# Holding back the first output stores until the input loads are through, in a 3x3 convolution

## Chip, cores, metric

The kernel runs on one core of one Trainium2 chip; the other cores are idle. The metric is the device time of one execution in microseconds (us). The "span" of a profile runs from the first to the last instruction and is about 1.8 us shorter than the device time of the same run. The "granted clock" is the share of its full speed at which TensorE was allowed to run. HBM is the chip's large memory, SBUF the memory beside the engines, and PSUM the one that TensorE writes its products to. For a program on one core, a run is called slow when it is over 1.5% above the fastest run of the same kernel; ratios use the other runs, called fast.

## The reference

A convolution of 16 images, 64 input channels, 64x64 pixels, with 128 output channels and a 3x3 kernel, in fp32, zero padding. The weights are 90% zeros, but neither kernel uses that.

```python
batch, c_in, h, w, c_out, k = 16, 64, 64, 64, 128, 3
for b in range(batch):
    for co in range(c_out):
        for ci in range(c_in):
            for kh in range(k):
                for kw in range(k):
                    output[b, co] += weight[co, ci, kh, kw] * x_pad[b, ci, kh:kh+h, kw:kw+w]
```

Input 16.8 MB, output 33.6 MB: every byte has to cross between HBM and SBUF once.

## The kernel before

Images go in pairs (64 channels each fill 128 partitions). All eight pairs are loaded up front by GpSimd, cast to bf16 on the way; the first half of pair 0 (the "head") comes as fp32 by the sync queue and is cast on chip, so that TensorE can start early. Before it, 27 matmuls of zeros keep TensorE busy.

```python
xs = [x_pool.tile([128, H, W], BF16, name=f"x{p}") for p in range(NP)]
w_sb = const_pool.tile([C_OUT, C_IN * KH * KW], FP32, name="w_sb")
nc.sync.dma_start(out=w_sb, in_=weight.rearrange("o i kh kw -> o (i kh kw)"))
x_head = o_pool.tile([128, H, W], FP32, name="o")            # o_pool: 7 buffers of 16 KiB per partition
nc.sync.dma_start(out=x_head[:, 0:HEAD, :], in_=pair(0)[:, 0:HEAD, :])
nc.gpsimd.dma_start(out=xs[0][:, HEAD:H, :], in_=pair(0)[:, HEAD:H, :])
...
for p in range(1, NP):
    nc.gpsimd.dma_start(out=xs[p], in_=pair(p))
...
for _ in range(27):
    nc.tensor.matmul(idle_ps, idle_rhs, idle_rhs, start=True, stop=True)
```

A block is 16 rows of a pair. GpSimd adds neighbouring rows ("row sums", s), TensorE makes 6 + 24 products, ScalarE copies the shared ones out of PSUM, and VectorE (DVE) adds them to the rest into the output buffer. After a pair's four blocks two stores of 2 MiB are issued.

```python
def twos(p, o, r0):
    s = s_pool.tile([128, 8, W], BF16, name="s")              # s_pool: 3 buffers
    nc.gpsimd.tensor_tensor(out=s, in0=..., in1=..., op=ADD)
    shared = product([(s, G1, 0, 1)], 8)
    ...
    for first, terms in ((r0, even), (r0 + 1, odd)):
        ps = product(terms, 8)
        for n in range(2):
            nc.vector.tensor_tensor(out=o[n][:, first : r0 + 16 : 2, :], in0=ps[n], in1=pc[n], op=ADD)

for p in range(NP):
    o = [o_pool.tile([C_OUT, H, W], FP32, name="o") for _ in range(2)]
    ...                                                       # four blocks; the last pair stores in halves
    if not last:
        for n in range(2):
            nc.sync.dma_start(out=out[2 * p + n], in_=o[n])
```

## Time and profile before

| | before |
|---|---|
| device time | 127.76 us, median of 3 (127.69 to 127.97) |
| span of the profile | 125.4 us (this run took 127.12 us) |
| TensorE busy | 107.5 us (86%), matmuls to 110.4 us |
| VectorE, GpSimd, ScalarE busy | 66%, 32%, 31% |
| DMA engines | 8 or 9 tenths busy in all slices but the first and the last |
| stores issued | 18, the first at 21.6 us, the last at 111.8 us |

### The profile page before, as it was taken

Reading aid. Unit: us, or ns where it says so; the run is one execution under the profiler, and the core shown is the slowest. Engines: PE = TensorE matmul, PEld = TensorE weight load, DVE = VectorE, ACT = ScalarE, POOL = GpSimd, SP = SyncE. Lnnn points to the kernel's source line nnn. Section 1 sums busy time; section 2 is a strip of 40 time slices with the busy share of each in tenths; the row PEclk is TensorE's granted clock in tenths of the full one; section 3 lists DMA queues with packets and bytes.
Section 4 is the critical chain, followed back from the end, with each engine's and each line's share of the span. In section 5 each row is a group of like instructions: output and inputs, shape, how many; then the busy total and the mean of one; then the engine's idle time right before and its main releaser. Section 6 shows DMA issues by size and latency. Waiting matters only on the chain.

```text
span 125.4 us, 2486 instructions
## 1 busy us (share of the span) xinstructions
PE 107.5 (86%) x1002; PEld 58.8 (47%) x1002; DVE 82.4 (66%) x135; ACT 39.0 (31%) x71; POOL 40.7 (32%) x45
## 2 busy tenths in 40 slices
PE   6679999999999999999999999999999999920000
PEld 6435555555555555555555555555555555500000
DVE  0463877877787778777877787778777877760000
ACT  4555323333333333333333333333333333300000
POOL 6936533333333333333333333333333300000000
PEclk9999999999999999999999999999999999997555
DMA  5999999989999999999999999999999999999980
GB/s 146 338 222 220 212 214 220 191 259 350 324 311 337 308 293 319 342 316 308 426 429 423 408 429 434 450 416 434 418 418 429 429 444 423 434 397 423 423 369 10
DMA packets 4044, 42.93 MB, mean 342 GB/s; under 512 B 448, under 2 KB 448, under 8 KB 704
## 3 DMA queue, kind: packets, MB, share of 16 engines
q1 hardware_dynamic: 2880, 34.90, 66.2%
q0 software_dynamic: 1152, 7.86, 30.7%
q8 instruction: 8, 0.13, 0.4%
q14 instruction: 4, 0.03, 0.1%
HBM read 17.07 MB, written 33.55 MB: 404 GB/s over the span
## 4 chain that ended last, share of the span: by engine, by line
PE 81%; DMA 4%; DVE 1%; issue 1%; DVEq 0%; SPq 0%
PE ps L135 81%; DMA o<-in_x_dram 4%; DVE o L168 1%; DVEq L214 0%; DVE x L87 0%; SPq L60 0%; DVEq L168 0%
## 5 line engine op out<-in xcount | busy, mean ns | idle before, releaser
L168 DVE TENSOR_TENSOR o<-ps,pc 128x512 f32<-128x512 f32 x124 | 77.8, 686 | 22.1 <-PE ps L135 19.8
L135 PE MATMUL ps<-x,wT 64*128 64x504 bf16 (+3 forms) x780 | 88.8, 373 | 1.5 <-DVE x L87 1.5
L135 PEld LDWEIGHTS <-wT 64*128 64x128 bf16 x966 | 55.2, 94 | 49.4 <-issue 1.5
L154 POOL TENSOR_TENSOR s<-x 128x512 bf16<-128x512 bf16 x31 | 35.6, 1152 | 57.7 <-PE ps L135 41.5
L161 ACT COPY pc<-ps 128x512 f32<-128x512 f32 x62 | 33.3, 589 | 64.0 <-issue 61.8
L135 PE MATMUL ps<-s,wT 64*128 64x512 bf16 (+1 forms) x186 | 25.7, 377 | 0.0
L74 PE MATMUL ps<-idle_rhs 128*128 128x128 bf16 x27 | 3.1, 310 | 1.0 <-DVE idle_rhs L71 1.0
L67 POOL DMA_DIRECT2D x<-in_x_dram x7 | 3.7, 561 | 0.0
L74 PEld LDWEIGHTS <-idle_rhs 128*128 128x128 bf16 x27 | 2.8, 144 | 1.0 <-DVE idle_rhs L71 1.0
L91 DVE CAST w_bf<-w_sb 128x192 bf16<-128x192 f32 (+1 forms) x4 | 1.3, 382 | 3.0 <-DMA w_sb<-in_weight_dram 3.0
L149 DVE COPY o<-ps 128x512 f32<-128x512 f32 x2 | 1.4, 692 | 2.0 <-PE ps L135 2.0
L148 ACT COPY o<-ps 128x512 f32<-128x512 f32 x2 | 1.2, 586 | 2.4 <-PE ps L135 2.4
L87 ACT CAST x<-o 128x576 bf16<-128x576 f32 (+1 forms) x2 | 1.5, 802 | 0.5 <-DMA o<-in_x_dram 0.5
L91 ACT ACT_TABLE_LOAD x1 | 1.3, 1283 | 0.7 <-PEq L203 0.7
L97 PE MATMUL ps<-ident,w_bf 128*128 128x128 bf16 x9 | 1.1, 292 | 0.4 <-DVE w_bf L91 0.4
L87 DVE CAST x<-o 128x576 bf16<-128x576 f32 x1 | 0.5, 460 | 1.4 <-DMA o<-in_x_dram 1.4
L91 ACT CAST w_bf<-w_sb 128x64 bf16<-128x64 f32 (+1 forms) x2 | 0.7, 418 | 1.9 <-DMA w_sb<-in_weight_dram 1.9
L97 PEld LDWEIGHTS <-w_bf 128*128 128x128 bf16 x9 | 0.8, 128 | 0.8 <-DVE w_bf L91 0.8
L101 DVE TENSOR_TENSOR wT<-ps,wT 128x384 bf16<-128x384 f32 x2 | 1.0, 550 | 0.0
L63 POOL DMA_DIRECT2D x<-in_x_dram x1 | 0.7, 696 | 0.8 <-POOLq L203 0.8
L71 DVE MEMSET idle_rhs<- 128x64 uint32 x1 | 0.1, 112 | 0.8 <-PEq L203 0.8
L110 ACT CAST wT<-ps 128x384 bf16<-128x384 f32 x1 | 0.5, 481 | 0.4 <-PE ps L97 0.4
(8 smaller groups left out, 1.9 us busy)
## 6 DMA issues: line engine op xcount, KB each, us to landing
out_dram<-o SPq DMA_DIRECT2D x14, 2048.0 KB, 19.8
x<-in_x_dram POOLq DMA_DIRECT2D x7, 1024.0 KB, 29.3
out_dram<-o SPq DMA_DIRECT2D x4, 1024.0 KB, 12.3
o<-in_x_dram SPq DMA_DIRECT2D x1, 1024.0 KB, 5.4
x<-in_x_dram POOLq DMA_DIRECT2D x1, 512.0 KB, 7.5
w_sb<-in_weight_dram SPq DMA_DIRECT2D x1, 288.0 KB, 3.1
```

Source lines behind the costliest of these rows:

```text
L67: nc.gpsimd.dma_start(out=xs[p], in_=pair(p))
L74: nc.tensor.matmul(idle_ps, idle_rhs, idle_rhs, start=True, stop=True)
L87: copy(out=xs[0][:, a:b, :], in_=x_head[:, a:b, :])
L91: copy(out=w_bf4[:, g, a:b, :], in_=w_v[:, k : k + b - a, :])
L97: nc.tensor.matmul(wps[:, j, :], src, ident, start=True, stop=True)
L101: nc.vector.tensor_tensor(out=wT[:, g], in0=wps, in1=wT[:, G1], op=SUB)
L135: nc.tensor.matmul(ps[n][:, lo:hi, c_lo:c_hi], tap(g, kw, n), src[q, a:b:step, c_lo + kw - 1 : c_hi + kw - 1], start=(i == 0), stop=(i == ...
L148: nc.scalar.copy(out=o[0][:, r0 : r0 + rows, :], in_=ps[0])
L149: nc.vector.tensor_copy(out=o[1][:, r0 : r0 + rows, :], in_=ps[1])
L154: nc.gpsimd.tensor_tensor(out=s, in0=xs[p][:, r0 : r0 + 16 : 2, :], in1=xs[p][:, r0 + 1 : r0 + 16 : 2, :], op=ADD)
L161: nc.scalar.copy(out=c, in_=shared[n])
L168: nc.vector.tensor_tensor(out=o[n][:, first : r0 + 16 : 2, :], in0=ps[n], in1=pc[n], op=ADD)
```

## The change

The intent: let the loads have the DMA engines to themselves first, and only then the stores. The stores of pairs 0 and 1 are held; the first of them gets an artificial dependency on the last addition of the second block of pair 2 (pairs are counted from 0), and the others stand behind it on the sync queue. As three pairs must now fit on chip before the first store, there are eight output buffers instead of seven. The room comes from putting the fp32 weights into the unused half of the head's buffer and from having two row-sum buffers instead of three.

```diff
--- before.py
+++ after.py
@@ -42,9 +42,9 @@
 
     const_pool = ctx.enter_context(tc.tile_pool(name="const", bufs=1))
     x_pool = ctx.enter_context(tc.tile_pool(name="x", bufs=1))
-    s_pool = ctx.enter_context(tc.tile_pool(name="s", bufs=3))
+    s_pool = ctx.enter_context(tc.tile_pool(name="s", bufs=2))
     p_pool = ctx.enter_context(tc.tile_pool(name="pc", bufs=4))
-    o_pool = ctx.enter_context(tc.tile_pool(name="o", bufs=7))
+    o_pool = ctx.enter_context(tc.tile_pool(name="o", bufs=8))
     psum_pool = ctx.enter_context(
         tc.tile_pool(name="psum", bufs=8, space=bass.MemoryType.PSUM)
     )
@@ -56,10 +56,12 @@
         return x[2 * p : 2 * p + 2].rearrange("n i h w -> (n i) h w")
 
     xs = [x_pool.tile([128, H, W], BF16, name=f"x{p}") for p in range(NP)]
-    w_sb = const_pool.tile([C_OUT, C_IN * KH * KW], FP32, name="w_sb")
+
+    first_buf = o_pool.tile([128, H, W], FP32, name="o")
+    x_head = first_buf[:, 0:HEAD, :]
+    w_sb = first_buf.rearrange("p h w -> p (h w)")[:, HEAD * W : HEAD * W + C_IN * KH * KW]
     nc.sync.dma_start(out=w_sb, in_=weight.rearrange("o i kh kw -> o (i kh kw)"))
-    x_head = o_pool.tile([128, H, W], FP32, name="o")
-    nc.sync.dma_start(out=x_head[:, 0:HEAD, :], in_=pair(0)[:, 0:HEAD, :])
+    nc.sync.dma_start(out=x_head, in_=pair(0)[:, 0:HEAD, :])
     nc.gpsimd.dma_start(out=xs[0][:, HEAD:H, :], in_=pair(0)[:, HEAD:H, :])
     ident = const_pool.tile([128, 128], BF16, name="ident")
     make_identity(nc, ident)
@@ -165,9 +167,18 @@
         for first, terms in ((r0, even), (r0 + 1, odd)):
             ps = product(terms, 8)
             for n in range(2):
-                nc.vector.tensor_tensor(
+                done = nc.vector.tensor_tensor(
                     out=o[n][:, first : r0 + 16 : 2, :], in0=ps[n], in1=pc[n], op=ADD
                 )
+        return done
+
+
+
+    HELD = 2
+    held = []
+
+    def store(p, n, o, a, b):
+        return nc.sync.dma_start(out=out[2 * p + n][:, a:b, :], in_=o[n][:, a:b, :])
 
     for p in range(NP):
         o = [o_pool.tile([C_OUT, H, W], FP32, name="o") for _ in range(2)]
@@ -175,17 +186,30 @@
         for blk in range(4):
             r0 = 16 * blk
             if BLOCKS[p][blk] == "T":
-                twos(p, o, r0)
+                done = twos(p, o, r0)
             else:
                 for r, rows in ((r0, 8), (r0 + 8, 8)):
                     direct(p, o, r, rows)
             if last and blk % 2 == 1:
                 for n in range(2):
-                    rows = slice(r0 - 16, r0 + 16)
-                    nc.sync.dma_start(out=out[2 * p + n][:, rows, :], in_=o[n][:, rows, :])
-        if not last:
+                    store(p, n, o, r0 - 16, r0 + 16)
+            if p == HELD and blk == 1:
+                first = store(*held[0])
+                tc.add_manual_dep(
+                    first.ins,
+                    done.ins.name,
+                    mybir.DependencyInfo(
+                        mybir.DependencyClass.Sync, mybir.DependencyReason.DATA
+                    ),
+                    reason="loads first",
+                )
+                for args in held[1:]:
+                    store(*args)
+        if p < HELD:
+            held += [(p, n, o, 0, H) for n in range(2)]
+        elif not last:
             for n in range(2):
-                nc.sync.dma_start(out=out[2 * p + n], in_=o[n])
+                store(p, n, o, 0, H)
 
 
 # ---- launch: one core; inputs and outputs as the reference has them ----
```

## The prediction

> **What bounds the kernel now.** I read the chain of work that ended last first, because it names an engine, and then the slices, because they say whether that engine reaches the end of the span. The columns of the first two lines are shares of the span.
>
> ```profile
> PE 81%; DMA 4%; DVE 1%; issue 1%; DVEq 0%; SPq 0%
> PE   6679999999999999999999999999999999920000
> DVE  0463877877787778777877787778777877760000
> DMA  5999999989999999999999999999999999999980
> GB/s 146 338 222 220 212 214 220 191 259 350 324 311 337 308 293 319 342 316 308 426 429 423 408 429 434 450 416 434 418 418 429 429 444 423 434 397 423 423 369 10
> ```
>
> The chain puts 81% on the matmuls of line 135, but it stops at 111.8 us, with the last DVE addition and the last store's issue, while the span is 125.4 us. In the last four slices (each 3.13 us) PE and DVE are at 0 and the DMA row is still at 9. So the last 12 us are stores draining. The DMA row is at 8 or 9 from the second slice to the last but one: the 16 DMA engines never run dry after the first 3 us. I take the DMA queue as the bound and PE as second, some 12 us behind.
>
> The GB/s row seems to say otherwise: 215 at first, 320 in the middle, 427 late. The load queue writes bf16 and is counted by the bytes that it writes, while it reads fp32. The queues in four stretches show it (8 to 22, 22 to 26, 26 to 60 and 64 to 110 us; packets, MB, share of the 16 engines' time; q0 carries the loads that cast, q1 the stores):
>
> ```profile
> q0 software_dynamic: 411, 3.02, 103.4%
> ...
> q0 software_dynamic: 99, 0.68, 99.8%
> q1 hardware_dynamic: 3, 0.05, 2.9%
> ...
> q1 hardware_dynamic: 489, 7.23, 50.7%
> q0 software_dynamic: 483, 3.56, 50.1%
> ...
> q1 hardware_dynamic: 1339, 19.58, 100.0%
> ```
>
> Counting a load's bytes twice (fp32 read), loads alone move 2 x 3.02 MB / 14 us = 431 GB/s. Loads and stores mixed move (2 x 3.56 + 7.23) / 34 = 422. Stores alone move 19.58 / 46 = 426. The rate is thus the same whatever the mix, and only the total counts. The one worse stretch is 22 to 26 us, just after the first store is issued at 21.6 us: (2 x 0.68 + 0.05) / 4 = 353 GB/s. Against 431 that is 0.31 MB short, or 0.7 us. The trace's packet records show load packets of 0.62 us stretching to 0.8 to 1.3 us there, and the first store packet only at 25.8 us, 4.2 us after its issue.
>
> **What the Trainium skill says.** "DMA: Bandwidth & Descriptors", section "Where 436 GB/s comes from", gives the 16 SBUF ports a ceiling of 435.2 GB/s. The trace agrees: 422 to 431 in the three steady stretches, so there is almost nothing left to gain in rate. The same page, "Issuing engines are not separate DMA queues", says that DMAs from the sync and gpsimd engines run on the same 16 engines and interleave; the trace agrees with 50.7% and 50.1% for the two queues while both have work. Holding the stores back then frees the loads but does not shorten the sum. "SBUF — State Buffer", section "SBUF size: 192, 224, or 256?", gives about 208 KiB usable per partition. The eight inputs take 64 KiB, eight output buffers 128, the four fp32 copies 8, two row sums 2, and the constants some 5.5 (0.25 + 0.25 + 1.5 + 3.75, rounded): 208. That is why the weights move into the first output buffer and one row-sum buffer goes. No timing follows from it, and no run here shows the limit.
>
> **The change part by part.**
> 1. Row sums in two buffers. GpSimd's addition of 1152 ns (31 of them) can start once the shared product two blocks back has read its buffer. That product is the first 6 matmuls of a block, done about 0.83 us into it (the timeline shows 6 in 0.83 us). So the sum is ready about 0.83 + 1.15 + 0.1 = 2.1 us into block k for block k+2. A block lasts 12.8 us / 4 = 3.2 us (stores of successive pairs are issued at 34.35 and 47.15 us), so it is wanted at 6.4 us. 4.3 us of slack: cost 0.
> 2. Weights in the output buffer. The weight load and the head of x go to disjoint columns of one tile. That disjoint regions of a tile do not wait for one another shows today: the casts write rows 0 to 31 of the first input at 6.6 us, and its lower half, loaded by another DMA, lands only at 1.24 + 7.5 = 8.7 us. So the start should not move: PE at 7.1 us, and cost 0.
> 3. Eight buffers. Buffer reuse moves from three and a half pairs back to four. Pair 4 first writes at about 61.1 us. If the stores begin at 43 us, pair 0's 4.19 MB are out at 43 + 9.8 = 53, with a couple of us for the receipt 55. Pair 5 (73.9 us) needs pair 1, out at 63 to 65; pair 6 (86.7) pair 2, at 72 to 75; pair 7 (99.5) pair 3, at 82 to 84. No wait, slack 6 us or more; PE should still end at 110.4 us.
> 4. The held stores. Pair 0 has three blocks of sums and pair 1 four, so the addition that releases the first store is number 12 + 16 + 8 = 36 of line 168. In the DVE timeline:
>
> ```profile
> 38.76 2.52 DVE L168 TENSOR_TENSOR o<-ps,pc 128x512 f32<-128x512 f32 x4 [0.73 <-PE ps L135]
> 42.00 2.52 DVE L168 TENSOR_TENSOR o<-ps,pc 128x512 f32<-128x512 f32 x4 [0.73 <-PE ps L135]
> ```
>
> It ends at 38.76 + 2.52 = 41.3 us, so the first store is issued at 41.3 instead of 21.6. The loads meanwhile have the engines alone. By 22 us they have moved 3.59 of 7.86 MB. The other 4.27 MB at 3.02 / 14 = 0.216 MB per us take 19.8 us, so the loads end at about 41.8 us, and a little later with the stragglers (in the packet records some engines run 0.5 us behind), instead of 61.8. They were not late before: PE ran without a gap from 7.1 us on, and GpSimd waited for a load once, 2.2 us. Nothing is bought by having them earlier.
>
> Then only stores: 33.55 MB / 0.426 = 78.8 us. The end of the stream is the time of the first store byte plus 78.8 us. That first byte lies between 41.3 + 1.1 = 42.4 us (the first load is issued at 0.74 us and its first packet is at about 1.85, queue empty) and 41.3 + 4.2 = 45.5 us (the latency seen behind a full load queue). The loads run out just then, so I choose near the low end, 43.2 us: end of the stream at 122.0 us. Today's stream ends at 121.9 in the mean (120 us, then 2 us at 87%, then 3.4 us at 5%), with one straggling engine to 123.7. The sum: the 0.7 us handover slump goes away or shrinks, a gap of about 1 us between loads and stores comes in its place, and the mixing loss (422 against about 428 over 34 us, 0.5 us at most) goes as well. **Net about 0**, 127.8 us.
>
> **The rivals.**
> - A, an idle gap. If the first store needs its 4.2 us whatever the load queue does, the engines idle from 42 to 45.5 us, and the stream ends at 45.5 + 78.8 = 124.3, 2.4 us later: 130.1 us. For it: 4.2 us is the only store latency that can be read, as all later stores queue behind others. Against it: about six load packets of 0.62 us ahead in each engine would explain 3.7 us of it, and the first loads took 1.1 us.
> - B, separate streams are better. If mixing is what costs, the slump of 0.7 us and the mixed loss of 0.5 us are both saved, and the store stream starts at 42.4: 126.6 us. For it: the slump is real. Against it: more than that cannot come, since the total of 50.6 MB at 431 is 117.4 us and the engines are already busy nearly all the time.
> - C, PE becomes the end. It would if a buffer or the weights' shared tile stalled it: a false wait of the weight casts for the head of x (lands at 6.6 us, weights at 3.9) would push PE and thus the release back by up to 2.7 us, and the gap would grow by as much: 130 us. Against it: point 2.
>
> **Range and chances.** The middle is 127.8. Rival B gives the low side, so 126.9; the high side takes two thirds of rival A, so 129.3. Faster by over 2% (under 125.2 us) would take more than all idle and mixed loss that I can count: 0.03. Slower by over 2% (over 130.3 us) takes the full gap plus something: 0.06. Within 2%: 0.91.
>
> **What would show it.** Right: slices with 210 to 220 GB/s to about 42 us, then 427 to the end, without a 320 stage; first store issued at 41.3; PE without a gap and its end at 110.4; the DMA end within 1 us of 122. Rival A: one slice near 41 to 45 us with a DMA share well under 9. Rival C: DVE or PE waiting for the weights or for stores, and PE's start later than 7.1 us. The prediction is wrong if stores alone right after the loads run at a rate clearly off 426, or if the slowest engine's straggling (1.5 us today) changes much.

## The result and the profile after

| | before | changed |
|---|---|---|
| device time, same rounds | 127.77 us median of 6 (127.63 to 129.78) | 129.51 us median of 6 (128.87 to 133.74) |
| ratio of fast runs | 1 | 1.013, 95% interval 1.009 to 1.017 |
| span of the profile | 125.4 us | 128.0 us |
| first store issued | 21.6 us | 43.8 us |

A ratio is the mean time of one kernel's fast runs over the mean of the other's fast runs of the same rounds, so it is not quite the ratio of the medians in the table; the slowest run of each kernel here (129.78 and 133.74 us) is slow by the rule above and left out of it. The changed kernel is 1.3% slower. The forecast was 127.8 us with a range to 129.3: the time is outside of it, though only by 0.2 us, and "within 2%" came true.

These lines are of the page of the changed kernel: busy tenths of PE, granted TensorE clock and busy tenths of the DMA engines in 40 slices of 3.2 us, what the DMA engines moved (loads counted by the bf16 bytes that they write), and the chain of work that ended last (DVEq and SPq are the sequencers of VectorE and of the sync queue).

```profile
PE   6659999999999999999999999999999999920000
...
PEclk9985999999999999999999999999999999999555
DMA  4999999999999399999999999999999999999970
GB/s 119 356 227 210 210 225 215 212 207 230 212 210 215 123 415 410 410 410 456 428 410 410 425 456 415 404 415 430 448 410 425 410 456 415 425 392 417 425 315 15
...
PE 81%; DMA 5%; DVE 1%; issue 1%; DVEq 0%; SPq 0%
```

Three things differ from the lines of before. The DMA row has a 3 in the fourteenth slice (41.6 to 44.8 us), with 123 GB/s: a hole. The GB/s row has no 320 stage any more: about 215 to the hole, then about 425. And the clock row has an 8 and a 5 in the third and fourth slice. The chain is again PE with 81% and again says nothing on the end, which is 14 us of draining stores.

The queues of the changed kernel, from 8 to 42 us and from 46 to 110 us (packets, MB, share of the 16 engines' time):

```profile
q0 software_dynamic: 1002, 7.30, 102.8%
...
q1 hardware_dynamic: 1854, 27.05, 100.2%
```

The loads alone move 2 x 7.30 MB / 34 us = 429 GB/s, the stores alone 27.05 / 64 = 423, against 431 and 426 before. Then four stretches of 2 us around the hole in the changed kernel; the last three columns are the granted clock, the DMA share and GB/s:

```profile
core 0: us, PE busy (x) PEld busy (x) DVE busy (x) ACT busy (x) POOL busy (x), PEclk, DMA share, GB/s
40.00:42.00 2.00, 2.00 (x22) 0.99 (x18) 1.27 (x3) 0.97 (x2) 1.15 (x1) 1.00 0.96 201
42.00:44.00 2.00, 2.00 (x22) 1.01 (x20) 1.74 (x3) 0.86 (x2) 0.77 (x1) 1.00 0.15 33
44.00:46.00 2.00, 2.00 (x22) 1.05 (x20) 1.54 (x3) 0.21 (x1) 0.38 (x1) 1.00 0.82 344
46.00:48.00 2.00, 2.00 (x22) 1.03 (x20) 1.27 (x3) 1.07 (x2) 1.15 (x1) 1.00 1.06 442
```

From 42 to 44 us the engines are 15% busy, then 82%: about 2 x 0.85 + 2 x 0.18 = 2.1 us of all 16 engines are lost. The packet records say that the last load packet ends at 43.4 us (on the slowest engine; most are done by 42.3) and that the first store packet starts at 44.68 us. All compute engines work on in this time. And the release comes late. This is the DVE line of the additions, the fourth of which frees the first store, in the changed kernel:

```profile
41.22 2.52 DVE L170 TENSOR_TENSOR o<-ps,pc 128x512 f32<-128x512 f32 x4 [0.72 <-PE ps L137]
```

It ends at 41.22 + 2.52 = 43.7 us, where the same addition of the profile before ended at 41.3. The 2.5 us are there from the start of the kernel on. The first real matmuls, before:

```profile
7.12 3.99 PE L135 MATMUL ps<-x,wT 64*128 64x512 bf16 x36 [1.54 <-DVE x L87]
10.93 0.83 PE L135 MATMUL ps<-s,wT 64*128 64x512 bf16 x6
```

and changed:

```profile
7.90 5.67 PE L137 MATMUL ps<-x,wT 64*128 64x512 bf16 x36 [2.39 <-DVE x L89]
13.39 0.83 PE L137 MATMUL ps<-s,wT 64*128 64x512 bf16 x6
```

The second line of each is the first matmul of the next block, and it starts 2.46 us later in the changed kernel (13.39 against 10.93). Of this, 0.78 us is the later start, as the matmuls wait for the cast of the head (7.90 against 7.12). The other 1.68 us is in the 36 matmuls themselves, which spread over 5.5 instead of 3.8 us: the clock record has half clock from 8.78 to 12.19 us, 3.41 us in which half the speed costs 1.7 us.

### The profile page after: what moved, and what is told of

Its sections match the earlier page's. It is cut to its first block, busy times and chain, and to the rows that moved or that the text cites. A ratio compares the mean times of both kernels' runs of the same rounds, so it can differ in the third digit from the quotient of the medians.

```text
span 128.0 us, 2487 instructions
## 1 busy us (share of the span) xinstructions
PE 109.2 (85%) x1002; PEld 57.3 (45%) x1002; DVE 82.3 (64%) x135; ACT 38.9 (30%) x71; POOL 40.8 (32%) x45
## 3 DMA queue, kind: packets, MB, share of 16 engines
HBM read 17.07 MB, written 33.55 MB: 396 GB/s over the span
## 4 chain that ended last, share of the span: by engine, by line
PE 81%; DMA 5%; DVE 1%; issue 1%; DVEq 0%; SPq 0%
PE ps L137 81%; DMA o<-in_x_dram 5%; DVE o L170 1%; DVEq L238 0%; DVE x L89 0%; SPq L63 0%; DVEq L170 0%
## 5 line engine op out<-in xcount | busy, mean ns | idle before, releaser
L137 PE MATMUL ps<-x,wT 64*128 64x504 bf16 (+3 forms) x780 | 90.3, 379 | 2.4 <-DVE x L89 2.4
L137 PEld LDWEIGHTS <-wT 64*128 64x128 bf16 x966 | 53.8, 95 | 53.4 <-issue 4.0
L163 ACT COPY pc<-ps 128x512 f32<-128x512 f32 x62 | 33.3, 589 | 64.0 <-issue 61.8
L93 DVE CAST w_bf<-o 128x192 bf16<-128x192 f32 (+1 forms) x4 | 1.1, 352 | 2.8 <-DMA o<-in_weight_dram 2.8
L93 ACT CAST w_bf<-o 128x64 bf16<-128x64 f32 (+1 forms) x2 | 0.7, 414 | 1.7 <-DMA o<-in_weight_dram 1.7
```

Of the source, the lines that this page charges most:

```text
L93: copy(out=w_bf4[:, g, a:b, :], in_=w_v[:, k : k + b - a, :])
L137: nc.tensor.matmul(ps[n][:, lo:hi, c_lo:c_hi], tap(g, kw, n), src[q, a:b:step, c_lo + kw - 1 : c_hi + kw - 1], start=(i == 0), stop=(i == ...
L163: nc.scalar.copy(out=c, in_=shared[n])
```

## The experiments

At this point there were two theories. **Gap**: the 1.3% is DMA idle time between the end of the loads and the first store, and the release comes late because TensorE did. **Rate**: stores alone are slower than stores mixed with loads, and the time of the release does not matter. Beside them stands the question whether the late start is chance or is made by the change (the shared buffer). All runs gave correct results.

### e1: everything but the held stores

```diff
-    HELD = 2
+    HELD = 0
-            if p == HELD and blk == 1:
+            if held and blk == 1:
```

> All of the change except the held stores: eight buffers with the weights in the first, two row sums, stores issued when ready as before. Gap theory (the 1.3% is DMA idle time between the end of the loads and the first store): no gap can arise, so the time of before, 127.8 us, ratio 0.995 to 1.005. Start theory (the shared buffer makes the head of x land late, 7.4 instead of 6.6 us, and PE then starts late): PE starts near 7.9 us here too; if that alone costs the time, 129 us or more. If PE starts at 7.1 us, the late head of the changed kernel's profile was chance or comes from elsewhere.

Measured: 127.88 us median (127.68 to 128.71), ratio 1.003 (1.000 to 1.005). Buffers, weights and row sums together cost nothing that can be told from zero. In the profiled run the head of x was ready even later, at 8.25 us, and the clock fell too, so that TensorE ended 4.5 us later than in the first profile of before; that run took 128.71 us. The DMA engines of that run at 98 to 102 and 102 to 106 us:

```profile
98.00:102.00 4.00, 4.00 (x42) 2.05 (x39) 3.27 (x6) 1.07 (x2) 1.15 (x1) 1.00 0.93 393
102.00:106.00 4.00, 4.00 (x42) 2.05 (x40) 3.41 (x7) 1.10 (x3) 1.16 (x1) 1.00 0.71 295
```

With TensorE that late, the store queue runs dry near 102 us (shares 0.93 and 0.71) and some 1.4 us are lost (4 x 0.07 + 4 x 0.29). So in a kernel that stores as early as it can, TensorE may be a little late for nothing, but not 4.5 us.

### e2 and e3: the release one block earlier and one block later

```diff
-            if p == HELD and blk == 1:
+            if p == HELD and blk == 0:      # e2
+            if p == HELD and blk == 2:      # e3
```

> The changed kernel with the release one block (3.2 us) earlier, after the first block of the third pair. Gap theory: first store issued at 38 to 40.6 us while loads still have 2 to 4 us to go, no idle slice, at most a slump like the 0.7 us one of before: 127.4 to 128.2 us. Rate theory (stores alone, in step over the 16 engines, are slower than mixed: 424 against 426 to 430 GB/s, and the slowest engine straggles more): release does not matter, 129.2 us or more.

Measured: 127.71 us median (127.55 to 128.34), ratio 1.000 (0.998 to 1.002). In e2 the hole is gone, at 42 to 44 and 44 to 46 us:

```profile
42.00:44.00 2.00, 2.00 (x22) 1.04 (x19) 1.27 (x3) 1.08 (x2) 1.15 (x1) 1.00 0.97 393
44.00:46.00 2.00, 2.00 (x22) 1.08 (x20) 2.00 (x4) 0.26 (x1) 0.16 (x1) 1.00 0.97 406
```

The first store of e2 was issued at 39.95 us and its first packet ran at 42.0, while loads ran to 44.9 us.

> The changed kernel with the release one block (3.2 us) later, after the third block of the third pair. Gap theory: the DMA gap grows by 3.2 us and the time with it, 132.5 to 133.0 us, ratio about 1.038. Rate theory: no change from 129.5 us. A buffer stall at pair 4 (first write at 61 to 63 us; pair 0 out at about 59) is not expected.

Measured: 132.67 us median (130.51 to 133.82), ratio of fast runs 1.027 (1.022 to 1.032). By the rule only the quickest of e3's runs count as fast, so the ratio is a low estimate, and the expected 1.038 was too high for it; the median is within the forecast. e3 from 42 to 50 us (its profile is used here only to see where the engines were idle):

```profile
42.00:44.00 2.00, 2.00 (x22) 1.02 (x20) 1.79 (x3) 0.00 (x0) 0.14 (x1) 1.00 0.15 33
44.00:46.00 2.00, 2.00 (x22) 0.97 (x18) 1.27 (x3) 1.07 (x2) 1.15 (x1) 1.00 0.00 0
46.00:48.00 2.00, 2.00 (x22) 0.97 (x19) 1.97 (x4) 0.63 (x2) 0.53 (x1) 1.00 0.00 0
48.00:50.00 2.00, 2.00 (x22) 1.07 (x20) 1.30 (x3) 0.45 (x1) 0.62 (x1) 1.00 0.62 262
```

The hole is now some 6.4 us by the packet records (5.5 us lost by 48 us and 0.9 more to the first packet): issue at 48.06 us, first packet at 48.91. That is about 4.1 us more than in the changed kernel's profile and not 3.2, as TensorE was 1.0 us later here as well. Moving nothing but the release by one block either way moved the ratio to before from 1.013 to 1.000 and to 1.027. The rate theory, which expected no movement, falls as the explanation of the whole; a smaller loss of rate is in the table below.

### e4: TensorE kept busy before the head arrives

```diff
     cast_x(nc.scalar.copy, 18, HEAD)
+    for _ in range(24):
+        nc.tensor.matmul(idle_ps, idle_rhs, idle_rhs, start=True, stop=True)
```

> The changed kernel with 24 more idle matmuls after the weight transposes, so that PE is not idle for 2.4 us before the first real matmul. Clock theory (the half clock of the changed kernel's start, and with it 1.7 us of the release's 2.4 us delay, comes from that idle stretch): granted clock 1.00 from 8 to 22 us, the 36th addition ends near 42.0 instead of 43.7 us, gap under 1 us, time 127.6 to 128.3 us. If the idle stretch has nothing to do with it: clock 0.88 again and 129.5 us.

Measured: 127.66 us median (127.56 to 128.34), ratio 1.000 (0.998 to 1.003). In e4 the first line below is the added matmuls, the second the first real ones, the third the next block:

```profile
5.27 2.13 PE L122 MATMUL ps<-idle_rhs 128*128 128x128 bf16 x24
7.33 3.99 PE L139 MATMUL ps<-x,wT 64*128 64x512 bf16 x36
11.15 0.81 PE L139 MATMUL ps<-s,wT 64*128 64x512 bf16 x6
```

The next block starts 3.8 us after the first real matmul, as in the full-clock profile of before; the release is at 41.6 us, the first store packet at 42.44. From 42 to 46 us:

```profile
42.00:44.00 2.00, 2.00 (x22) 0.94 (x20) 1.78 (x3) 0.00 (x0) 0.14 (x1) 1.00 0.95 365
44.00:46.00 2.00, 2.00 (x22) 0.89 (x18) 1.27 (x3) 1.07 (x2) 1.16 (x1) 1.00 0.99 418
```

So the whole 1.3% can be taken away on TensorE's side without touching the release.

The clock records also suggest why the half clock, though not the late head, is a matter of chance. All their stretches between two changes of clock are multiples of 3.413 us, and they begin at another time in each run. In the six falls to half clock that are recorded near the start (the changed kernel, e1, e2, e5, e6, e8), matmuls ran for 0.75 to 1.25 us of the last 3.41 us before the fall. In the first profile of before, the stretch from 5.34 to 8.75 us has 1.87 us of matmuls, and the clock stayed full; in e4 the one to 6.58 us has 3.22. So whether the clock fell seems to have hung on where the stretches happened to lie over the pause before the head, until e4 filled that pause. This is a regularity of these profiles; where the limit lies was not measured.

That e2 and e4, two unrelated edits, both arrive at the time of before is what the gap theory needs.

### e5: the same extra matmuls in the kernel before

The edit is that of e4.

> The kernel before with the same 24 idle matmuls. Theory (before, PE's start is hidden under the drain of the stores, so its clock and start cost nothing; only the held stores make the end depend on PE): 127.66 us, ratio 0.998 to 1.002. If the idle matmuls are a gain of their own that has nothing to do with the held stores, as e4 would then show: 126 us or less.

Measured: 127.40 us median (127.22 to 129.77), ratio 0.998 (0.994 to 1.001). Keeping TensorE warm (at full clock) is no gain of its own here; what e4 gained belongs to the held stores. One run (the profiled one) had its head only at 10.5 us and took 129.77 us. There the extra matmuls end at 6.6 us, the clock falls after all (half from 11.8 to 15.2 us), and the store queue runs dry (DMA share 0.41 from 102 to 106 us): a very late start hurts the kernel before as well, and the extra matmuls don't cure it.

### e6: weights in a buffer of their own

```diff
-    w_sb = first_buf.rearrange("p h w -> p (h w)")[:, HEAD * W : HEAD * W + C_IN * KH * KW]
+    w_buf = o_pool.tile([128, H, W], FP32, name="o")
+    w_sb = w_buf.rearrange("p h w -> p (h w)")[:, 0 : C_IN * KH * KW]
```

> The changed kernel with the weights in an output buffer of their own instead of the second half of the head's buffer (still eight buffers, no more memory). Chance theory (the head of x lands anywhere from 6.6 to 8.2 us in any of these kernels): the head lands in the same range and the time is that of the changed kernel, 128.8 to 129.8 us. Shared buffer theory (two transfers into one buffer delay the head): it lands at 6.6 us or earlier, PE starts at 7.1 us at full clock, and the time is that of e4, 127.6 us.

Measured: 130.46 us median (129.09 to 134.79), ratio 1.016 (1.010 to 1.022): nothing regained. The median lies above even the 128.8 to 129.8 us that the chance theory expected. In its profiled run the head came early (matmuls from 7.22 us), and yet the next block starts only 5.5 us after:

```profile
7.22 5.67 PE L138 MATMUL ps<-x,wT 64*128 64x512 bf16 x36 [2.13 <-DVE x L90]
12.71 0.83 PE L138 MATMUL ps<-s,wT 64*128 64x512 bf16 x6
```

That is the half clock alone, without a late head. The shared buffer is not the cause.

### e8: the kernel before, unchanged, profiled again

> The kernel before, unchanged, for a second profile of its start. Chance theory: the head of x may land at any time from 6.6 to 8.2 us and the clock may fall here too, at the same total time, 127.3 to 128.0 us. Shared buffer theory: it lands at 6.6 us again and the clock stays at 1.00.

Measured: one run, 127.72 us. Its first matmuls:

```profile
7.99 5.28 PE L135 MATMUL ps<-x,wT 64*128 64x512 bf16 x36 [2.80 <-DVE x L87]
13.09 0.82 PE L135 MATMUL ps<-s,wT 64*128 64x512 bf16 x6
```

The kernel before also starts late (7.99 us) at half clock, with the next block at 13.09 us, 2.2 us later than in its first profile, and it still takes 127.72 us. This shows two things: a late start at half clock comes without the change too, and the kernel before pays at most 0.6 us for 2.2 us of it (127.72 against the 127.12 us of the first profiled run). As a single run it doesn't show how often each kernel starts late. But of the nine profiles without extra matmuls only that first one had its 36 matmuls done in 3.8 us; the other eight took 5.1 to 6.7 us, as at half clock for most of that time.

### e7: released by a load instead of an addition

```diff
-        nc.gpsimd.dma_start(out=xs[p], in_=pair(p))
+        load = nc.gpsimd.dma_start(out=xs[p], in_=pair(p))
+        if p == NP - 2:
+            gate = load
...
-                    done.ins.name,
+                    gate.ins.name,
```

> The changed kernel with the first store waiting for the landing of the last but one load instead of an addition of the third pair, so that PE's late start can't delay it. That load lands near 39 us, the last one runs another 4.5 us, so no idle slice whatever the clock. Gap theory: 127.4 to 127.9 us, with PE starting late or not, and little spread. If a late PE costs the changed kernel time by another way (buffers, a late end of the matmuls), 128.5 us or more.

Measured: 127.89 us median (127.42 to 130.96), ratio 0.998 (0.994 to 1.003). The profiled run had a late TensorE (7.85 us, half clock; matmuls to 113.7 us), but the store was issued at 38.91 us, and from 42 to 46 us there is no hole:

```profile
42.00:44.00 2.00, 2.00 (x21) 0.96 (x18) 1.89 (x4) 0.00 (x0) 0.04 (x1) 1.00 0.97 360
44.00:46.00 2.00, 2.00 (x22) 1.01 (x20) 1.27 (x4) 1.07 (x2) 1.15 (x1) 1.00 1.02 418
```

The small spread that I expected did not come: two of six runs were slow (130.31 and 130.96 us). I have no trace of them. In the profiled run the queue runs partly dry near 100 us as in e1, so a late TensorE has a second way to cost time that no release mends. Whether that made the two slow runs is not shown.

### e9 and e10: both repairs together, and the changed kernel again

e9 has the edits of e4 and e7; e10 is the changed kernel, unchanged, on the same chip.

> Both repairs together: the first store waits for the last but one load (as in e7) and 24 idle matmuls keep the clock (as in e4). If the handover slump of before (0.8 us lost between 22 and 40 us) is all that loads first can save, and the overlap near 40 us costs 0.2 to 0.6 us, then 127.0 to 127.6 us, ratio 0.995 to 1.000: no real gain over before. A ratio under 0.99 would mean that loads first has a gain that the gap had covered.

> The changed kernel, unchanged, beside e9 on the same chip. Gap theory: its single times spread with PE's start, from 127.7 us (release near 41.5 us, no late head) to 130 us, median 129 to 129.8, ratio 1.010 to 1.016; in the profile, first store packet 0.85 us after the issue, and idle time from the end of the loads to it.

Measured: e9 127.81 us median (127.42 to 130.96), ratio 0.999 (0.995 to 1.003); e10 130.24 us (129.11 to 130.56), ratio 1.017 (1.012 to 1.021). e10 repeats the result, a little worse than the first time and than expected (129 to 129.8 us, ratio 1.010 to 1.016); no single run came near the 127.7 us that it expected of one with an early start, the quickest took 129.11. The repaired version beats the changed kernel by 2.4 us and does not beat the kernel before. No kernel here does.

### The profiles side by side

From the packet records, per profiled run. "Lost" is the time in which 16 engines at 430 GB/s (loads counted by fp32 bytes) would have moved what was not moved. "16 KiB" is the mean time of a full store packet from 62 to 95 us.

| kernel | first real matmul | first store issued | its first packet | last load packet ends | lost 22-48 us | lost 48-95 | lost 95-120 | 16 KiB, ns | span |
|---|---|---|---|---|---|---|---|---|---|
| before | 7.12 | 21.60 | 25.76 | 61.8 | 0.95 | 0.22 | 0.16 | 615 | 125.4 |
| before again (e8) | 7.99 | 23.76 | 27.74 | 60.2 | 1.21 | 0.21 | 0.18 | 615 | 125.9 |
| changed | 7.90 | 43.83 | 44.68 | 43.4 | 2.31 | 0.68 | 0.41 | 620 | 128.0 |
| changed again (e10) | 7.29 | 44.22 | 45.06 | 43.4 | 2.75 | 0.68 | 0.41 | 620 | 128.4 |
| e1 not held | 8.76 | 26.11 | 30.52 | 57.7 | 0.98 | 0.22 | 1.90 | 614 | 126.9 |
| e2 earlier | 7.26 | 39.95 | 42.04 | 44.9 | 0.23 | 0.18 | 0.53 | 614 | 125.8 |
| e3 later (slow run) | 8.17 | 48.06 | 48.91 | 44.2 | 5.50 | 1.69 | 0.36 | 620 | 132.0 |
| e4 warm | 7.33 | 41.59 | 42.44 | 43.7 | 0.34 | 0.62 | 0.39 | 620 | 125.8 |
| e5 warm before (slow run) | 11.05 | 27.21 | 31.17 | 58.3 | 0.89 | 0.36 | 2.75 | 615 | 128.0 |
| e6 own buffer | 7.22 | 43.15 | 43.99 | 43.6 | 1.69 | 0.68 | 0.41 | 620 | 127.3 |
| e7 by load | 7.85 | 38.91 | 42.06 | 44.7 | 0.61 | 0.21 | 1.20 | 615 | 126.2 |
| e9 by load, warm | 7.25 | 38.98 | 42.05 | 45.2 | 0.41 | 0.17 | 0.20 | 614 | 125.8 |

The three "lost" columns add up to 1.33 us before and 3.40 us changed. The difference of 2.07 us is most of the 2.6 us between the spans; 1.36 us of it is the hole less the handover slump of before, and 0.71 us (0.68 - 0.22 and 0.41 - 0.16) is a slower store stream. Of the remaining 0.5 us, 0.13 lies before 22 us; most of the rest is in the tail, where the last store packet ends 2.2 us after the mean end of the stream (126.40 against 124.2 us) instead of 1.8 (123.74 against 121.9). Beside e8, a more usual run of the kernel before, the changed kernel's sum is 1.80 us higher and its span 2.1 us.

## Why the prediction was wrong, point by point

- **The bound** was named rightly: DMA traffic, and not PE with its 81% of the chain. In e8 TensorE is 2.2 us late, and the time is 127.72 us, at most 0.6 us more.
- **"The rate is the same whatever the mix"** holds to 1.5%: 429, 423 and 426 GB/s. But the 0.426 MB per us that I used for the stores became 0.423 to 0.424. Over 33.55 MB that is 0.4 to 0.6 us, in the direction of slower.
- **"It ends at 38.76 + 2.52 = 41.3 us, so the first store is issued at 41.3"** is the step that failed. I took one profile's time of an addition as a property of the kernel. The profile was of the quickest run, and its time the earliest of all twelve profiles: in the eight later profiles without extra matmuls (e1, e2, e3, e6, e7, e8 and the two of the changed kernel) the same addition ended 1.8 to 4.5 us later, at 43.1 to 45.8 us. Issue came at 43.8 us (and 44.2 us in the repeat). Point 2, "PE at 7.1 us, and cost 0", has the same fault: the shared buffer does cost 0 (e1, e6, e8), but the start is not 7.1 us. I had written that PE is hidden, and did not see that the change ends just this: it ties the start of the store stream, which is on the path, to TensorE, which was not.
- **The first store's latency**: the low end, 1.1 us, was the right choice over the 4.2 us of rival A, and was 0.85 us (43.83 to 44.68). The first packet came at 44.7 instead of my 43.2 us, 1.5 us later: the release cost 2.5 us, and a latency of 0.85 instead of the 1.9 us that 43.2 allows for gave 1.0 back. With 0.4 to 0.6 us of rate that makes 1.9 to 2.1 us of the 2.2 by which the stream ended late; the mean end of the stream was 124.2 us (120 us, then 1.03 x 2, 0.85 x 2 and 0.10 x 4) and not 122.0.
- **Rival A** gave nearly the right time, 130.1 us, with the wrong mechanism: the gap is there, but from a late release and not from a long latency. **Rival C** had a late TensorE in it, but by a false wait, which e6 and e8 exclude. **Rival B** fell: e2, e4, e7 and e9 have no hole, and none is faster than before.
- **Where the hoped-for gain went**: the slump at the handover does go away, as foreseen (nothing is lost from 22 to 40 us in the changed kernel). e9 gets 0.95 us of loss down to 0.41 us. Even so its span is no shorter than that of before: 0.5 us of saved transfer in a stream of 120 us doesn't show in the time.
- **Buffers and row sums**: no wait, as worked out. e1 shows it for the time, and the matmuls of the changed kernel run without a gap from 7.9 us on.
- **Slips that decide nothing**: the constants of the SBUF sum are 5.75 and not 5.5 KiB, the last four digits of the DMA row are 9, 9, 8 and 0, the slowest engine straggles 1.8 and not 1.5 us (123.7 against 121.9), and rival B's own start of 42.4 us gives an end 0.7 us earlier, so 127.1 us, where 126.6 counts the saving twice.

What stays open: why the head of x comes anywhere between 6.6 and 10.5 us, why stores are some 1% slower in some kernels (below), and the slow runs of e7 and e9.

## What to carry to other kernels

Before you tie a transfer to an engine's progress, ask whether that engine was off the path: an artificial wait puts all of its chance delays onto the path. Release by what you really wait for, here a load, or let the two phases overlap by more than the spread. Where the same DMA engines are busy from end to end, reordering transfers can gain only what the order itself wastes, and here that was under 1% (the 0.95 us lost at the handover in a span of 125.4). And read more than one profile before a forecast hangs on the time of a single instruction.

## What the Trainium skill lacked or had wrong

- "DMA: Bandwidth & Descriptors", section "Latency and other measured facts", gives about 600 ns to the first byte for sync-queue DMAs. Here it was 0.85 us with the engines empty, but 2.1 us (e2), 3.2 us (e7) and 4.2 us (before) with loads queued; a figure for a loaded queue is missing.
- No page that I read has it that a whole store stream can run 1% slower than another: full packets took 620 ns in the five profiles whose first store packet came 0.85 us after the issue, and 614 or 615 ns in the seven in the table whose first packet came 2.1 to 4.4 us after it, among loads. That is a regularity of twelve profiles; its cause was not tested.
- "TensorE: Matmul & The Clock Gate", Part 1, is right that the window of about 3.4 us is free-running and the cold start varies from run to run: half-clock stretches of 3.41 us are in the clock records of the changed kernel and of e8, and the same 36 matmuls took 3.8 us in one profile of the kernel before and 5.1 us in the other. For a forecast it says only that the ramp costs under 1% of a typical span and that one should not fit to one count of slow matmuls. What it lacks is a case like this, where a transfer waits for TensorE: 1.7 us of half clock is two thirds of a delay that made the kernel 1.3% slower, and with a late head added, an addition's time read off a single profile was 1.8 to 4.5 us too early for the others. Its caveat that clock events in a trace are not to be trusted alone fits too: in e10 the clock row shows no fall, and yet the first 36 matmuls took 6.5 us (the next block at 13.78, the first at 7.29). That trace holds no clock record before 12.77 us, so the nines of the row before it measure nothing; e3 and e7 begin at 13.1 and 13.2 us in the same way.
